# Expert layer: the 160-slot unit is fed one block at a time between blocks of the 64-slot units

## The chip, the cores and the metric

One core of one Trainium2 chip runs the whole program. The metric is the device time of one execution in microseconds (us). Before the change the median of 3 runs is 1689.62 us (1689.18 to 1689.63). The engines are named as the profile names them: PE (TensorE, the matrix engine; PEld is its loading of the stationary operand), DVE (VectorE), ACT (ScalarE), POOL (GpSimd) and SP (SyncE, which here only issues DMAs).

## The reference, cut to what matters

Two layers: each has a token mixer and a channel mixer. The second layer's channel mixer sends each of 256 tokens to 2 of 8 experts; each expert is a SwiGLU with three 1024 x 3584 matrices in float32. The change lies entirely in this part.

```python
def swiglu(y, wg, wu, wd):
    return (jax.nn.silu(y @ wg) * (y @ wu)) @ wd

def moe_swiglu(y, w_r, b_r, wg, wu, wd):
    logits = (y @ w_r).astype(jnp.float32) + b_r.astype(jnp.float32)
    top_val, top_idx = lax.top_k(logits, TOP_K)
    gates = jax.nn.softmax(top_val, axis=-1)
    combine = jnp.sum(jax.nn.one_hot(top_idx, N_EXPERTS, dtype=jnp.float32)
                      * gates[..., None], axis=-2).astype(y.dtype)
    out = jnp.zeros_like(y)
    for e in range(N_EXPERTS):
        out = out + combine[..., e:e + 1] * swiglu(y, wg[e], wu[e], wd[e])
    return out
...
f = ffn(modulate(rmsnorm(h, g_ffn_pre[i]), sh_f, sc_f))
h = h + gt_f * rmsnorm(f, g_ffn_post[i])
```

## The kernel before, in words

**Units.** The eight experts are worked through as eight units. Unit 0 is expert 0 with 32 slots for tokens; the other seven are sorted at run time by how many tokens chose them and get the fixed sizes of `SLOTS`: unit 1 has 160 slots, units 2 and 3 have 96, units 4 to 6 have 64, unit 7 has 32. In `SEQ` the first number is the rank (0 is the 160-slot unit, 3 to 5 the 64-slot units, 6 the last 32-slot unit, None is expert 0); below, units are named by their slots. Tokens beyond the slots are caught by code behind a branch that is not entered here.

**Blocks.** The 3584 hidden columns are cut into 7 blocks of 512 (`EB`). For each unit and block SP loads three tiles of 2 MiB ("quads"): two of gate and up weights (`eg`, `eu`), one of down weights (`ed`). So there are 56 blocks and 168 quads. `SEQ` lists runs of blocks, `(unit, first, end)`; `moe_items` (L1817) turns it into the order of the loads, always the gate and up quads of one block and then the down quad of the block before it. `t_load` (L475) issues them from SP in this order, each one when a buffer is free. There are eight buffers of this size (`NS`, `KEEP`); `REST` (L59) sets, at a step counted in blocks, how many of them are kept back for converted weights: 3 from step 7, none from step 28.

**Two ways to multiply.** 128 slots of the 160 go the "narrow" way: ACT and DVE split each weight quad into a rounded part and a rest (`t_hi`, `t_lo`, two further buffers a quad), and PE makes three fp32r products 128x512 for each (`mm3`), in `t_egu` (L1529) and `t_edown` (L1568). Slots in parts of 64 or 32 go the "wide" way, `t_xgu` (L1692) and `t_xdown` (L1733): raw float32 weights, two or four products side by side in the array, each shown as two MATMUL instructions. The last 32 of the 160 slots and the second part of each 96-slot unit are such parts of 32.

**Accumulators and finishes.** The sum over the blocks of one run of `SEQ` stays in PSUM banks (two for 128 slots, one for each wide part). At the end of the run a finish (`t_finish` L1589, `t_xfinish` L1758) splits it on ACT and DVE, multiplies it by the one-hot matrix on PE and adds it on DVE to the output `facc` by token. So a unit that is cut in three runs has three finishes. There are eight PSUM banks: `b:acc` accumulators, `b:g` gate and up, `b:m` (at most two) transposes and gathers, `b:x` the finish.

**The order on the engines.** The Python program plays a model of the engines (`Sched`, `Eng.product` holds the PE costs): of the tasks that could start it takes the one that starts first, with small biases. The order in which PE, ACT, DVE and SP get their instructions is that order. All engines' instructions are recorded on one line (L307), so rows are told apart by tile: `w` is a quad, `f`, `q`, `s` are smaller tiles, `b` a PSUM bank.

Of the kernel before, what the change touches and what calls it, by code (L numbers as in the profile page):

```python
# [17 lines left out]
F32R = mybir.dt.float32r  # L18
# [3 lines left out]
OP = mybir.AluOpType  # L22
# [7 lines left out]
EB = FF // 512  # L30
# [9 lines left out]
KEEP, SLACK, NEAR = 9, 4.0, 2  # L40
# [15 lines left out]
TABLE = 1.3  # L56
SC = {'PE': 1.0, 'ACT': 1.0, 'DVE': 1.0, 'POOL': 0.918, 'DMA': 1.0, 'NONE': 1.0}

REST = (0, ((6, 9, 0), (7, 9, 3), (28, 9, 0)))  # L59
ORD = ((1, 0, 5, 6, 7, 4, 3, 2, 8, 9, 10, 11), (5, 3, 2, 4, 6, 7, 9, 10, 8, 11, 0, 1))  # L60
CAP = (3, 1, 2, 4)
ADB, HI0 = -0.7, 5
# [8 lines left out]
JO = (3, 6, 1, 2, 5, 7, 4, 0)  # L71
WO = ((0, 2), (0, 1, 2, 3), (0, 1, 2, 3, 4, 6))

SEQ = ((None, 0, 7), (0, 0, 2), (3, 0, 7), (0, 2, 4), (4, 0, 7), (0, 4, 7), (5, 0, 7), (1, 0, 7), (6, 0, 4), (2, 0, 7), (6, 4, 7))


PE, ACT, DVE, POOL, DMA, NONE = "PE", "ACT", "DVE", "POOL", "DMA", "NONE"


def on(eng, *res, ev=()):  # L80

    return eng, res, tuple(ev)
# [213 lines left out]
class Eng:  # L296
# [17 lines left out]
    def product(self, op, out, a, n):  # L314
        if op == "transpose":
            return 0.11
        dt = a[1].dtype
        if dt == F32R and self.s.change and a[0].shape[0] < 128:
            return n / 2400 * a[0].shape[0] / 128 + 0.03
        if dt == F32R:  # L320
            return n / 2400 + 0.003 if n >= 256 else max(n / 600, 0.03)
        if out.shape[0] == 32:
            return max(n / 2300, 0.055)
        if out.shape[0] == 64 and n >= 256:
            return n / 1100
        return max(n / 600, 0.06) if dt == F32 else max(n / 2400, 0.03)
# [46 lines left out]
class Core:  # L373
# [1254 lines left out]
    def experts(self, units, seq):  # L1628

        go = self.sc.spawn  # L1630
        prev, state, near = None, {}, []
        for key, b0, b1 in seq:
            _, pos, base, slots, comb = units[key]
            down = []
            parts = self.parts(slots)
            for s, ws in parts:
                if b0 == 0:
                    out, hts = [[Event(), Event()], [Event() for _ in ws or [128]]], [Event() for _ in range(EB)]
                    ev = near if prev is None else [*near, *prev] if key >= NE else [*near, *prev, self.combed]
                    go(self.t_xgather(key, pos, base + s, ws, out, ev) if ws else self.t_gather(key, pos, base + s, [out[0], out[1][0]], ev), -0.3)  # L1640
                    prev = out[0]
                    state[key, s] = out, hts
                out, hts = state[key, s]
                acc = [Event() for _ in ws or [128]]
                down.append((self.t_xdown(key, b0, b1, ws, hts, acc) if ws else self.t_edown(key, b0, b1, hts, acc[0]), 0.0))
                for i, w in enumerate(ws or [128]):
                    finish, a = self.t_xfinish if ws else self.t_finish, (comb, acc[i], out[1][i], b1 == EB, *([w] if ws else []))
                    if (key, b0, b1) == seq[-1] and key < NE and (s, ws) == parts[-1] and i == len(ws or [128]) - 1:

                        self.last = lambda done, f=finish, a=a: f(*a, done)  # L1650
                    else:
                        down.append((finish(*a), -0.2))
            for b in range(b0, b1):
                for s, ws in reversed(parts):
                    out, hts = state[key, s]
                    go(self.t_xgu(key, b, ws, out[0], hts[b]) if ws else self.t_egu(key, b, out[0], hts[b]))
            if self.facc is None:
                self.facc = []
                go(self.t_facc([hts[3]]))
            near = [hts[max(b0, b1 - NEAR)]]  # L1660
            if (key, b0, b1) == seq[-1] and key < NE:
                go(self.t_gate([self.colev[1, 5], hts[max(b0, b1 - 3)]]))
            for t in down:
                go(*t)
# [93 lines left out]
    def t_xfinish(self, comb, acc, oht, last, w, done=None):  # L1758
        n = 8 * w
        fs = yield on(ACT, *["hr:xf"] * (w // 32), ev=[acc])  # L1760
        own = list(fs) if w == 64 else [fs]
        fs = self.pair(n, own)
        yield from self.g_split(acc.v[:, :n], *fs)
        self.sc.rel(acc.v)
        yield on(PE, ev=[oht, self.combed, self.faccev])
        comb = comb()
        ps = yield on(PE, *["b:x"] * 4)
        at = lambda t, q: (ps[2 * t + q], slice(0, 512)) if w == 64 else (ps[q], slice(t * 256, t * 256 + 256))
        for t in range(2):
            for i in range(2):  # L1770
                for q in range(128 // w):
                    r, (p, c) = slice(q * w, q * w + w), at(t, q)
                    self.pe.matmul(p[:, c], oht.v[r, t * 128:t * 128 + 128], fs[i][r, :], start=i == 0, stop=i == 1)
        for t in range(2):
            for q in range(128 // w):
                if q * n % 512 == 0:
                    yield on(DVE)
                f, (p, c) = self.facc[t][:, q * n:q * n + n], at(t, q)
                self.v.scalar_tensor_tensor(f, p[:, c], comb[:, t:t + 1], f, op0=OP.mult, op1=OP.add)
                if t or w == 64:  # L1780
                    self.sc.rel(p)
                if done and q * n % 512 + n == 512:
                    self.sc.set(done[t][q * n // 512])
        self.sc.rel(*own)
        if last:
            self.sc.rel(oht.v)
# [21 lines left out]
    @staticmethod  # L1808
    def seq():
        return [(0 if r is None else r + 1, b0, b1) for r, b0, b1 in SEQ]  # L1810

# [5 lines left out]
    def moe_items(self, seq, idx=None):  # L1817
# [16 lines left out]
        for n in range(len(steps) + 1):  # L1834
            if n < len(steps):
                e, b = steps[n]
                if idx is None:
                    it += [("rest", None, (r, q)) for m, r, q in REST[1] if n == m]
                for n2, k in enumerate(GU):
# [94 lines left out]
    def main(self):  # L1934
# [82 lines left out]
        self.sc.cap.update({("s", "raw"): 40, ("s", "hi"): 5, ("s", "lo"): 5})  # L2017
        self.sc.rest = REST[0]
        self.sc.change, self.sc.stay = CHG, STAY
# [136 lines left out]
```

## Time and profile before

| | |
|---|---|
| median of 3 runs | 1689.62 us |
| the profiled execution | 1687.98 us, of which the span in the trace 1685.9 us |
| PE busy | 1589.4 us (94%) |
| DVE, ACT busy | 775.9 us (46%), 528.6 us (31%) |
| moved by DMA | 497.30 MB, mean 295 GB/s |

How to read it: the expert layer is the second half of the span. By the trace, expert 0 (32 slots) ends at about 905 us, the 160-slot unit and the three 64-slot units fill 905 to 1360 us, and the 96-slot units with the last 32-slot unit fill the rest. The profiled execution is 1.64 us below the median of the runs. "Busy" of PE has modelled ends, so that consecutive matmuls overlap a little; intervals from start to start are the better price.

### The profile page before, as it was taken

The page shows a single profiled execution, that of the slowest core. Times are in us where ns is not written, and L with a number is a line of the kernel's source. Part 1 is how long each engine was busy: PE and PEld are TensorE (multiplying, and loading weights), DVE is VectorE, ACT ScalarE, POOL GpSimd, SP SyncE. Part 2 cuts the span into 40 slices and gives each one's busy share as a digit, 9 for nine tenths or more (in the row PEclk, how much of TensorE's full clock was granted, in tenths as well). Part 3 has the DMA queues.
Part 4 walks back from the last instruction along what each step waited for, and adds up shares of the span by engine and source line. Part 5 has one row for each costly group of instructions (what it writes and reads, how often), then busy time and mean ns, then how long its engine had stood idle before and what let it go on. Part 6 is the DMA issues. An engine that isn't in the chain of part 4 may idle for free. (4 is left out here: it accounts for less than half of the span.)

```text
span 1685.9 us, 25712 instructions
## 1 busy us (share of the span) xinstructions
PE 1589.4 (94%) x10580; PEld 1029.2 (61%) x10580; DVE 775.9 (46%) x1470; ACT 528.6 (31%) x951; POOL 26.2 (2%) x49
## 2 busy tenths in 40 slices
PE   6999999999999999999989999998999989989994
PEld 3776889888888888897646634642673333443342
DVE  4576688765644458987524512620841110021012
ACT  3477453323222235557415302410720000000001
POOL 0100000000000011000000000000000000000000
PEclk9999999999999999999989999999999999999997
DMA  9516435554544456864699999899889999999994
GB/s 370 212 37 238 167 133 209 180 171 152 178 159 163 171 187 208 317 245 142 261 374 418 385 427 425 367 426 428 331 338 428 426 426 427 391 425 427 426 425 180
DMA packets 71758, 497.30 MB, mean 295 GB/s; under 512 B 9004, under 2 KB 9136, under 8 KB 52048
## 3 DMA queue, kind: packets, MB, share of 16 engines
q1 hardware_dynamic: 68976, 490.76, 73.6%
q0 software_dynamic: 1792, 4.18, 0.7%
q8 instruction: 85, 1.39, 0.3%
q10 hardware_dynamic: 864, 0.62, 0.1%
q14 instruction: 41, 0.34, 0.1%
HBM read 494.49 MB, written 1.05 MB: 294 GB/s over the span
## 5 line engine op out<-in xcount | busy, mean ns | idle before, releaser
L307 PE MATMUL b<-s,s 128*128 128x512 f32 (+2 forms) x2864 | 579.7, 363 | 7.7 <-DVE s L307 6.5
L307 PEld LDWEIGHTS b<-s,s 128*128 128x128 f32 (+1 forms) x2864 | 460.1, 186 | 95.9 <-issue 9.6
L307 PE MATMUL b<-w,f 128*32 128x256 f32 (+1 forms) x2336 | 299.2, 480 | 28.9 <-DMA w<-in_w_gu_e_dram 28.9
L307 PE MATMUL b<-w,s 128*32 128x256 f32 (+2 forms) x1848 | 275.9, 439 | 9.1 <-DMA w<-in_w_gu_e_dram 9.1
L307 DVE TENSOR_TENSOR f<-f,b 128x256 f32<-128x256 f32 (+2 forms) x105 | 41.0, 393 | 518.3 <-ACT f L307 439.3
L307 ACT ACTIVATE f<-b 128x512 f32<-128x512 f32 (+4 forms) x183 | 82.3, 455 | 604.4 <-PE b L307 600.8
L307 PEld LDWEIGHTS b<-w,s 128*32 128x32 f32 (+2 forms) x1848 | 151.8, 138 | 123.3 <-issue 66.8
L307 PEld LDWEIGHTS b<-w,f 128*32 128x32 f32 (+1 forms) x2336 | 105.9, 124 | 197.9 <-issue 137.6
L307 ACT ACTIVATE s<-s 128x1024 fp32r<-128x1024 f32 (+2 forms) x173 | 179.0, 1050 | 146.8 <-PE b L307 84.4
L307 PE MATMUL b<-s,f 128*32 128x256 f32 (+1 forms) x1344 | 206.5, 401 | 16.7 <-DVE ones L774 8.6
L307 DVE TENSOR_TENSOR s<-s,s 128x1024 fp32r<-128x1024 f32 (+2 forms) x169 | 203.2, 1215 | 32.1 <-ACT s L307 27.9
L307 PEld LDWEIGHTS b<-s,f 128*32 128x32 f32 (+1 forms) x1344 | 145.0, 151 | 63.8 <-DMA s<-in_w_ada_dram 12.0
L307 DVE TENSOR_TENSOR w<-w,w 128x1024 fp32r<-128x1024 f32 x84 | 97.5, 1220 | 42.4 <-ACT w L307 42.3
L307 PE MATMUL b<-w,q 128*32 128x256 f32 (+1 forms) x880 | 111.5, 464 | 4.2 <-DMA w<-in_w_down_e_dram 2.2
L307 DVE SCALAR_TENSOR_TENSOR s<-s,cs,s 128x1024 f32<-128x1024 f32 x73 | 91.9, 1281 | 42.9 <-DMA s<-in_w_ada_dram 42.4
L307 ACT ACTIVATE w<-w 128x1024 fp32r<-128x1024 f32 x84 | 82.3, 1048 | 44.5 <-DMA w<-in_w_gu_e_dram 20.4
L307 PEld LDWEIGHTS b<-w,q 128*32 128x32 f32 (+1 forms) x880 | 39.3, 120 | 63.5 <-issue 53.2
L307 DVE TENSOR_TENSOR s<-b,s 128x512 f32<-128x512 f32 (+2 forms) x71 | 44.4, 629 | 54.5 <-ACT s L307 32.3
L307 PEld LDWEIGHTS b<-ident,f 128*128 128x128 f32 x313 | 34.2, 140 | 49.3 <-DVE f L307 22.5
L307 PE MATMUL b<-ident,f 128*128 128x128 f32 x313 | 55.3, 287 | 8.7 <-DVE f L307 4.6
L307 ACT ACTIVATE s<-b 128x512 f32<-128x512 f32 (+3 forms) x93 | 46.7, 524 | 46.9 <-PE b L307 44.9
L307 DVE SCALAR_TENSOR_TENSOR s<-b,utab,s 128x256 f32<-128x256 f32 (+1 forms) x88 | 44.2, 574 | 16.7 <-PE b L307 16.7
(162 smaller groups left out, 727.3 us busy)
## 6 DMA issues: line engine op xcount, KB each, us to landing
w<-in_w_gu_e_dram SPq DMA_DIRECT2D x101, 2048.0 KB, 20.9
w<-in_w_down_e_dram SPq DMA_DIRECT2D x52, 2048.0 KB, 21.7
s<-in_w_ada_dram SPq DMA_DIRECT2D x96, 512.0 KB, 4.8
s<-in_w_down_d_dram SPq DMA_DIRECT2D x56, 512.0 KB, 4.4
s<-in_w_gu_e_dram SPq DMA_DIRECT2D x44, 512.0 KB, 7.9
s<-in_w_gate_d_dram SPq DMA_DIRECT2D x28, 512.0 KB, 4.5
s<-in_w_up_d_dram SPq DMA_DIRECT2D x28, 512.0 KB, 3.9
s<-in_w_in_dram SPq DMA_DIRECT2D x24, 512.0 KB, 7.4
```

What stands on the lines that cost most here:

```text
L307: r = f(out, *a, **k)
```

## The change

The runs of `SEQ` are shorter: one block of the 160-slot unit stands between two or three blocks of the 64-slot units. The 160-slot unit keeps its accumulators over all seven blocks (`JOIN`) and is finished once instead of three times; each 64-slot unit is cut in three runs, with three finishes instead of one. The last 32-slot unit is cut in 2 + 2 + 3 blocks instead of 4 + 3, and comes earlier beside the 96-slot units. `t_xfinish` takes two banks `b:m` for each half of the tokens when the part has 64 slots, instead of four banks `b:x` at once. The reserve of buffers ends at step 32 instead of 28, and the planner's PE costs in this part are other ones.

```diff
-REST = (0, ((6, 9, 0), (7, 9, 3), (28, 9, 0)))
+REST = (0, ((6, 9, 0), (7, 9, 3), (32, 9, 0)))
...
-SEQ = ((None, 0, 7), (0, 0, 2), (3, 0, 7), (0, 2, 4), (4, 0, 7), (0, 4, 7), (5, 0, 7), (1, 0, 7), (6, 0, 4), (2, 0, 7), (6, 4, 7))
+JOIN = (1,)
+SEQ = ((None, 0, 7), (0, 0, 1), (3, 0, 3), (0, 1, 2), (3, 3, 6), (0, 2, 3), (3, 6, 7), (4, 0, 2), (0, 3, 4), (4, 2, 5), (0, 4, 5),
+       (4, 5, 7), (5, 0, 1), (0, 5, 6), (5, 1, 4), (0, 6, 7), (5, 4, 7), (6, 0, 2), (1, 0, 7), (6, 2, 4), (2, 0, 7), (6, 4, 7))
...
-        if dt == F32R and self.s.change and a[0].shape[0] < 128:
-            return n / 2400 * a[0].shape[0] / 128 + 0.03
+        if self.s.change:
+            if dt == F32R:
+                return n / 2400 * a[0].shape[0] / 128 + 0.016
+            if out.shape[0] < 128:
+                return n * out.shape[0] / 128 / 600 * 1.01
+            if n < 256:
+                return 0.225
...
+                if key in JOIN and b0:
+                    continue
+                d1 = EB if key in JOIN else b1
                 acc = [Event() for _ in ws or [128]]
-                down.append((self.t_xdown(key, b0, b1, ws, hts, acc) if ws else self.t_edown(key, b0, b1, hts, acc[0]), 0.0))
+                down.append((self.t_xdown(key, b0, d1, ws, hts, acc) if ws else self.t_edown(key, b0, d1, hts, acc[0]), 0.0))
...
-            near = [hts[max(b0, b1 - NEAR)]]
+            if key not in JOIN:
+                near = [hts[max(b0, b1 - NEAR)]]
...
-        ps = yield on(PE, *["b:x"] * 4)
-        at = lambda t, q: (ps[2 * t + q], slice(0, 512)) if w == 64 else (ps[q], slice(t * 256, t * 256 + 256))
-        for t in range(2):
-            for i in range(2):
-                for q in range(128 // w):
-                    r, (p, c) = slice(q * w, q * w + w), at(t, q)
-                    self.pe.matmul(p[:, c], oht.v[r, t * 128:t * 128 + 128], fs[i][r, :], start=i == 0, stop=i == 1)
...
+        for ts in ((0,), (1,)) if w == 64 else ((0, 1),):
+            ps = yield on(PE, *["b:m"] * 2 if w == 64 else ["b:x"] * 4)
+            for t in ts:
+                for i in range(2):
+                    for q, p in enumerate(ps):
+                        r = slice(q * w, q * w + w)
+                        self.pe.matmul(p[:, (t - ts[0]) * n:(t - ts[0]) * n + n], oht.v[r, t * 128:t * 128 + 128], fs[i][r, :],
+                                       start=i == 0, stop=i == 1)
+            for t in ts:
+                for q, p in enumerate(ps):
...
+                    self.v.scalar_tensor_tensor(f, p[:, (t - ts[0]) * n:(t - ts[0]) * n + n], comb[:, t:t + 1], f, op0=OP.mult, op1=OP.add)
+                    if t == ts[-1]:
+                        self.sc.rel(p)
```

## Rows read from the trace of the kernel before

**Rows 1.** The page, part 2: busy tenths in 40 slices of the span.
```profile
PE   6999999999999999999989999998999989989994
GB/s 370 212 37 238 167 133 209 180 171 152 178 159 163 171 187 208 317 245 142 261 374 418 385 427 425 367 426 428 331 338 428 426 426 427 391 425 427 426 425 180
```

**Rows 2.** Busy time by stretch: columns PE, PEld, DVE, ACT, POOL, clock, DMA share, GB/s.
```profile
905.00:960.00 55.00, 55.00 (x404) 37.09 (x397) 36.74 (x48) 26.61 (x35) 0.00 (x0) 0.98 0.95 387
960.00:1050.00 90.00, 84.34 (x432) 32.83 (x431) 17.06 (x28) 13.47 (x24) 0.00 (x0) 0.98 1.00 426
1050.00:1100.00 50.00, 50.00 (x332) 31.73 (x331) 30.52 (x39) 21.21 (x29) 0.00 (x0) 1.00 0.91 375
1100.00:1180.00 80.00, 73.73 (x366) 26.43 (x365) 10.29 (x21) 5.81 (x14) 0.00 (x0) 0.96 1.01 428
1200.00:1250.00 50.00, 50.00 (x361) 35.53 (x361) 34.28 (x44) 24.59 (x33) 0.00 (x0) 1.00 0.69 271
1250.00:1360.00 110.00, 102.34 (x546) 41.05 (x538) 18.56 (x36) 11.70 (x24) 0.00 (x0) 1.00 1.01 428
1450.00:1470.00 20.00, 20.00 (x230) 8.64 (x228) 0.98 (x3) 1.49 (x5) 0.00 (x0) 1.00 0.87 351
...
905.00:1360.00 455.00, 435.41 (x2559) 216.93 (x2551) 160.00 (x224) 115.85 (x172) 0.00 (x0) 0.99 0.95 399
...
1360.00:1659.00 299.00, 283.84 (x2811) 121.48 (x2811) 37.92 (x95) 23.49 (x66) 0.00 (x0) 0.98 0.99 420
```

**Rows 3.** The page, part 6: loads of weight quads, count, size, us to landing.
```profile
w<-in_w_gu_e_dram SPq DMA_DIRECT2D x101, 2048.0 KB, 20.9
```

**Rows 4.** PE in order of time: start, us to the last end, operation and count.
```profile
907.35 11.41 PE L307 MATMUL b<-w,s 128*128 128x512 f32 x48
918.69 1.93 PE L307 MATMUL b<-w,q 128*32 128x256 f32 x32
920.44 1.91 PE L307 MATMUL b<-w,f 128*32 128x256 f32 x32
922.28 0.66 PE L307 MATMUL b<-ident,f 128*128 128x128 f32 x4
...
984.45 1.89 PE L307 MATMUL b<-w,q 128*64 128x512 f32 x8
986.27 0.44 PE L307 MATMUL b<-ident,f 128*128 128x128 f32 x2
986.64 7.09 PE L307 MATMUL b<-w,f 128*64 128x512 f32 x32
```

**Rows 5.** Groups by shape from 905 to 1670 us: count, busy, mean ns, idle before.
```profile
L307 PE MATMUL b<-w,s 128*128 128x512 f32 x504 | 122.7, 398 | 0.0
...
L307 PE MATMUL b<-f,q 32*128 32x256 f32 x117 | 6.5, 317 | 4.2 <-ACT f L307 4.0
L307 PE MATMUL b<-s,q 128*128 128x512 f32 x24 | 6.3, 406 | 0.0
L307 PE MATMUL b<-f,q 64*128 64x512 f32 x40 | 5.9, 415 | 0.0
```

**Rows 6.** PE in order of time, where the tile forms alternate, 1216 to 1226 us.
```profile
1216.43 1.64 PE L307 MATMUL b<-w,s 128*128 128x512 f32 x6
...
1217.99 3.66 PE L307 MATMUL b<-w,f 128*32 128x256 f32 x64
...
1221.59 4.47 PE L307 MATMUL b<-w,s 128*128 128x512 f32 x18
```

**Rows 7.** Waits, 1195 to 1262 us: us in total, times, longest.
```profile
PEld b L307 <- issue: 9.2, 21, 0.8
```

**Rows 8.** Waits, 905 to 1360 us: us in total, times, longest.
```profile
PEld b L307 <- DVE f L307: 13.8, 19, 0.8
PE b L307 <- DMA w<-in_w_gu_e_dram: 17.2, 10, 4.1
```

**Rows 9.** SP's own waits, 905 to 1360 us.
```profile
SPq L509 <- PE b L307: 323.1, 82, 14.0
```

**Rows 10.** PE in order of time at the end: the last down block.
```profile
1661.99 1.93 PE L307 MATMUL b<-w,q 128*32 128x256 f32 x32 [1.76 <-SPq L1797]
```

More of the change, by code (lines that the diff above doesn't have):

```diff
@@ L1643, in experts @@
                 out, hts = state[key, s]
+                if key in JOIN and b0:
+                    continue
+                d1 = EB if key in JOIN else b1
                 acc = [Event() for _ in ws or [128]]
-                down.append((self.t_xdown(key, b0, b1, ws, hts, acc) if ws else self.t_edown(key, b0, b1, hts, acc[0]), 0.0))
+                down.append((self.t_xdown(key, b0, d1, ws, hts, acc) if ws else self.t_edown(key, b0, d1, hts, acc[0]), 0.0))
                 for i, w in enumerate(ws or [128]):
-                    finish, a = self.t_xfinish if ws else self.t_finish, (comb, acc[i], out[1][i], b1 == EB, *([w] if ws else []))
+                    finish, a = self.t_xfinish if ws else self.t_finish, (comb, acc[i], out[1][i], d1 == EB, *([w] if ws else []))
                     if (key, b0, b1) == seq[-1] and key < NE and (s, ws) == parts[-1] and i == len(ws or [128]) - 1:
@@ L1766, in t_xfinish @@
         comb = comb()
-        ps = yield on(PE, *["b:x"] * 4)
-        at = lambda t, q: (ps[2 * t + q], slice(0, 512)) if w == 64 else (ps[q], slice(t * 256, t * 256 + 256))
-        for t in range(2):
-            for i in range(2):
-                for q in range(128 // w):
-                    r, (p, c) = slice(q * w, q * w + w), at(t, q)
-                    self.pe.matmul(p[:, c], oht.v[r, t * 128:t * 128 + 128], fs[i][r, :], start=i == 0, stop=i == 1)
[L1774 to L1783, printed above, removed]
+        for ts in ((0,), (1,)) if w == 64 else ((0, 1),):
[8 more added lines that the diff above has]
+                for q, p in enumerate(ps):
+                    if q * n % 512 == 0:
+                        yield on(DVE)
+                    f = self.facc[t][:, q * n:q * n + n]
+                    self.v.scalar_tensor_tensor(f, p[:, (t - ts[0]) * n:(t - ts[0]) * n + n], comb[:, t:t + 1], f, op0=OP.mult, op1=OP.add)
+                    if t == ts[-1]:
+                        self.sc.rel(p)
+                    if done and q * n % 512 + n == 512:
+                        self.sc.set(done[t][q * n // 512])
         self.sc.rel(*own)
```

## The prediction

> **What bounds the kernel now.** Read the slices of the span first [rows 1]: in the second half, the expert layer, PE is busy at 8 to 9 tenths and DMA moves 418 to 428 GB/s in most slices, but not in all. So two engines share the bound, and the next view has to show which of them waits where. By stretch [rows 2] the two take turns. Where the 160-slot unit runs (905 to 960, 1050 to 1100, 1200 to 1250) PE has no idle time at all and DMA drops to 387, 375 and 271 GB/s. Where a 64-slot unit runs (960 to 1050, 1100 to 1180, 1250 to 1360) DMA is full at 426 to 428 and PE idles 5.7, 6.3 and 7.7 us; its waits there are for weights [rows 8], while SP's waits are nearly all for PE, which frees the buffers [rows 9].
>
> The prices say why. A block is three quads of 2 MiB [rows 3], 6.29 MB, 14.7 us at 427 GB/s. On PE, from start to start [rows 4], a 160-slot block costs 11.3 us (48 narrow products, gate and up), half of that again for down (5.7), twice 1.75 for the wide gate and up (64 instructions), 1.75 for wide down and 0.6 for transposes: 22.9 us, 8.2 more than its load. A 64-slot block costs 7.1 + 3.6 + 0.4 = 11.1 us, 3.6 less than its load. Two or three 160-slot blocks in a row put PE 16 to 25 us behind, the buffers fill, DMA stops; then seven 64-slot blocks make PE wait.
>
> Summed up: from 905 to 1360 us, 28 blocks that need 28 x 14.7 = 412 us of DMA take 455 us. DMA lacks (427 - 399) x 455 / 427 = 29.8 us there and (427 - 351) x 20 / 427 = 3.6 us at 1450 to 1470: 33.4 us. PE idles 455 - 435.4 = 19.6 us in this stretch and 299 - 283.8 = 15.2 us after it: 34.8 us. Neither is all to be had, but the time lies there.
>
> **The change part by part.** *Runs of one block.* One 160-slot block and three of 64 slots need 22.9 + 3 x 11.1 = 56.2 us of PE and 58.9 us of DMA, so within each group of four the excess of the one is paid by the other, and seven groups use up exactly the 7 and 21 blocks. The look-ahead is five quads (eight buffers, three kept back until step 32), 24.5 us, more than the 8.2 us that one 160-slot block puts PE behind. This takes away both waits as far as the rest of the work on PE allows, so PE's work is summed next.
>
> *Finishes.* Two of three finishes of the 160-slot unit go. In PE time: 2 x 8 products at 6.3 / 24 = 0.26 us and 2 x 16 at 6.5 / 117 = 0.056 us [rows 5], 4.2 + 1.8 = 6.0 us less. The 64-slot units have nine finishes instead of three: 6 x 8 products at 5.9 / 40 = 0.15 us, 7.1 us more; the last 32-slot unit has one more, 0.9 us. The splits and adds of these finishes lie on ACT and DVE, which are busy 115.9 and 160.0 of the 455 us [rows 2]: taken as hidden. If they were not, each finish would hold PE for one wait as in [rows 8], 13.8 / 19 = 0.73 us, 5 us in all.
>
> *More changes of tile form on PE.* 160-slot and 64-slot runs met 5 times in this stretch and will meet 13 times; where they meet, gate and up of the one alternate with down of the other, about four changes a time, so some 32 more. What one costs: six narrow products before a change took 1.56 us from start to start and 64 wide ones before the next 3.60 us [rows 6], against 1.42 and 3.50 us at the steady price of [rows 4]: 0.14 and 0.10 us. From above it is bounded by the loading of weights, which stood still 9.2 / 21 = 0.44 us each time without a reason shown [rows 7]; from below by 0, as PE itself shows no gap from 1200 to 1250. I take 0.14, the measured step: 4.5 us (0 to 14). The Trainium skill, page "TensorEngine Tiling (Array Packing)", section Tiling Modes, speaks against the change here: it says that a change of tiling mode, not of tile alone, drains the engine. It gives no price; with the upper bound as the drain the gain below would be 10 us smaller, and the 0.14 us say that most of the drain is hidden.
>
> *Two banks in place of four for a 64-slot finish, accumulators held throughout.* The 160-slot unit holds three of eight PSUM banks, now also while 64-slot blocks run. A 64-slot block then has its own accumulator and four others, a 160-slot block three for gate and up and one for transposes. No instruction is added. From below it may gain a little, since a finish no longer waits for four free banks; from above see the slower rival. I take 0.
>
> *Planner's costs and the reserve until step 32.* No instruction is added; they move only the order. Three buffers held back four steps longer shorten the look-ahead from 8 to 5 quads for blocks that are now interleaved. Bounds -3 to +3 us, 0 taken. SP's queue is in order: a late buffer holds back every load behind it, which is the second case below.
>
> *PE's clock.* It was granted 0.96 on the mean from 1100 to 1180 and 0.98 at 960 to 1050, the stretches with waits, that is the lower of its two levels for 8% and 4% of the time. Fewer waits can give back at most half of 6.4 + 3.6 us. I take 0, as these slow products lay beside waits for DMA.
>
> **The sum.** PE in the stretch of 28 blocks: 435.4 - 6.0 + 7.1 + 4.5 = 441 us. Some waiting will stay, between 0 (1200 to 1250) and 19.6 us; I take 3, since the groups are balanced to 5%. That is 444 in place of 455 us: 11 us. Behind it PE enters the 96-slot units with weights already there, since DMA, if it runs on, brings 444 / 14.7 = 30.2 blocks and the buffers hold 5 to 8 quads, 1.7 to 2.7 blocks, beyond the 28. Of the 15.2 us of PE waits after 1360, about half should go; the last blocks still wait for the last weights, and the down block at the end has its own 1.8 us wait [rows 10]. With the extra finish: 7 us. Together 18 us. The sum by DMA must agree: of 33.4 us missing, some 4 stay in the stretch, the 3.6 at 1450 to 1470 stay, and about 4 come new at the second 96-slot unit, where only two 32-slot blocks lie before it: 33.4 - 11.6 = 22 us. The smaller one governs. 1687.98 - 18 = 1670.0 us for the profiled execution, 1.64 more for the median: 1671.6 us. I predict 1671.5.
>
> **The rivals.** *The buffers still run full (1680 us, 20%).* A 160-slot quad needs its own buffer and two more for the split, and SP cannot pass it. Today DMA loses 29.8 / 7 = 4.3 us for each 160-slot block; if half of it stays, 15 us, then 33.4 - 15 - 7.6 leaves 11 us, less the tail that PE then brings: 8 to 10 us. For it: SP waited 323 us for PE in this stretch [rows 9]. Against it: the loss falls on runs of two and three such blocks, and grows with the run (387, 375, 271 GB/s).
>
> *PSUM becomes the bound (1705 us, 15%): slower.* In a 64-slot block only four banks are left for gate and up, transposes and finishes, and a 64-slot finish wants both `b:m` banks that transposes and gathers use. PE is in order, so a product that waits for a bank stops everything behind it, then SP's loads. One exposed wait for DVE cost 0.73 us [rows 8]. If each of 28 blocks loses one such wait and a form change of 0.44 us more, about 1.2 us, the sum is 33.6 - 18 = 15.6 us slower. It decides from 18 / 28 = 0.64 us a block on. Against it: PE waited for DVE only 19 times in 28 blocks, and the 160-slot blocks already ran with three accumulators held.
>
> *The order on PE does not change as `SEQ` does (within 0.2%, 8%).* PE's order is the planner's, not the list's; but the loads follow the list, so PE would then wait for them. Beyond my bounds, more than 28 us gained (all of PE's 34.8 us less the 6.5 added): 2%; a fault elsewhere that makes it slower: 1%.
>
> **How the numbers follow.** The forecast with its own range, 1661 to 1678 us (a gain of 12 to 28: form changes from 14 to 0 us, remaining waits 0 to 8), has 54%. About 0.2%, 3.4 us, is what can be told from no change. Faster: 54 + 20 + 2 = 76%; same 8%; slower 15 + 1 = 16%. The range goes from 1659 to 1692: it leaves out most of the slower case and next to nothing below.
>
> **What would show it.** Right: between 905 and 1350 us DMA above 415 GB/s with no slice under 350, PE idle under 8 us there, eight fp32r products of the narrow finish instead of 24, the last load some 18 us earlier and the same tail behind it. Wrong: many PE waits for DVE or ACT in 64-slot blocks (PSUM), or DMA still at 250 to 390 GB/s in steps of about 60 us (buffers), or PE slower at the same counts (form changes).

## The result and the profile after

The changed kernel takes 1664.34 us (median of 4 runs, 1662.94 to 1667.74) against 1689.4 us: ratio 0.9858, interval 0.984 to 0.9876, 25 us faster. The forecast was 1671.5 us, with its own range from 1661 to 1678. The profiled execution of the changed kernel took 1667.74 us, the longest of its four runs; against the profiled one before (1687.98 us) that is 20.2 us, so all comparisons of traces below explain 20 us and not 25; the other 5 are the spread of the runs on both sides.

The slices of the span, after (compare [rows 1]): from the 22nd slice to the last but one DMA is at 418 to 427 GB/s, with two dips left (397 and 391), and PE is at 8 or 9 tenths throughout.

```profile
PE   5999999999999999999998999999999999999995
GB/s 374 214 39 228 164 152 165 214 144 180 170 167 156 174 168 227 259 330 155 152 344 418 421 427 427 426 426 397 427 391 419 427 426 425 425 426 426 426 422 181
```

The same by stretch, with the columns of [rows 2]: PE, PEld, DVE, ACT, POOL, clock, DMA share, GB/s.

```profile
905.00:960.00 55.00, 54.37 (x392) 30.39 (x392) 21.68 (x31) 15.70 (x23) 0.00 (x0) 1.00 0.99 416
960.00:1050.00 90.00, 87.61 (x508) 42.60 (x506) 33.00 (x38) 26.88 (x38) 0.00 (x0) 1.00 1.01 426
1050.00:1100.00 50.00, 50.00 (x315) 24.75 (x312) 23.30 (x33) 14.53 (x20) 0.00 (x0) 1.00 1.01 426
1100.00:1180.00 80.00, 77.83 (x413) 37.21 (x415) 26.05 (x30) 21.42 (x31) 0.00 (x0) 0.96 0.98 412
1180.00:1260.00 80.00, 78.72 (x465) 39.74 (x459) 29.74 (x42) 18.47 (x28) 0.00 (x0) 1.00 0.97 408
1260.00:1350.00 90.00, 88.19 (x545) 41.71 (x543) 30.74 (x49) 19.78 (x32) 0.00 (x0) 1.00 1.00 423
...
1430.00:1450.00 20.00, 20.00 (x198) 8.03 (x197) 1.13 (x3) 1.54 (x4) 0.00 (x0) 1.00 1.01 428
...
905.00:1350.00 445.00, 436.71 (x2624) 216.39 (x2624) 164.50 (x220) 116.78 (x172) 0.00 (x0) 0.99 0.99 418
905.00:1640.00 735.00, 719.62 (x5364) 337.44 (x5366) 204.63 (x319) 140.23 (x237) 0.00 (x0) 0.99 1.00 420
```

No stretch swings between "DMA full, PE waits" and "PE full, DMA at 271" any more. DMA lacks (427 - 420) x 735 / 427 = 12.0 us from 905 to 1640, of them 9.4 up to 1350; before, the prediction's sum gave 33.4. PE idles 445 - 436.7 = 8.3 us up to 1350, the end of the interleaved part, and 15.4 us up to 1640; before it was 19.6 up to 1360 and 34.8 up to 1659, the same points of the work. PE's waits for gate and up weights in the interleaved part have shrunk from 17.2 us [rows 8] to 1.7, and DVE is now what PE waits for most (before, PE waited for DVE 1.0 us in all from 905 to 1659 us):

```profile
PE b L310 <- DVE f L310: 4.5, 5, 1.4
PE b L310 <- DMA w<-in_w_gu_e_dram: 1.7, 4, 0.6
```

How the blocks alternate on PE, after (start, us to the last end, operation, count): one block of narrow gate and up (48 products `w,s` 128*128), then 64-slot products (`w,q` and `w,f` 128*64), then the narrow down in pieces (18 of its 24) among them.

```profile
1157.87 11.37 PE L310 MATMUL b<-w,s 128*128 128x512 f32 x48
1169.17 1.08 PE L310 MATMUL b<-w,q 128*64 128x512 f32 x4
...
1173.07 6.18 PE L310 MATMUL b<-w,f 128*64 128x512 f32 x28
...
1183.09 4.46 PE L310 MATMUL b<-w,s 128*128 128x512 f32 x18
1187.48 3.65 PE L310 MATMUL b<-w,f 128*64 128x512 f32 x16
```

The end is the same work: the last down products, here two blocks of them, stop at 1643.92 + 3.66 = 1647.6 us, before at 1661.99 + 1.93 = 1663.9 [rows 10]; that is 16.3 us. From there to the end of the span it is 18.4 us instead of 22.0: the last finish now starts on ACT 0.1 us after these products and started 4.7 us after them before, by the trace without a reason shown.

```profile
1643.92 3.66 PE L310 MATMUL b<-w,q 128*32 128x256 f32 x64
```

Counted from the loads, the end is the same. The weight loads run out in the slice from 1655 to 1660 us before (first line) and in that from 1635 to 1640 after (second line), 20 us earlier, and the span is 1685.9 - 1666.0 = 19.9 us shorter.

```profile
1655.00:1660.00 5.00, 5.00 (x81) 3.01 (x73) 0.29 (x1) 1.04 (x3) 0.00 (x0) 1.00 0.73 310
1635.00:1640.00 5.00, 5.00 (x68) 2.62 (x70) 3.34 (x7) 0.60 (x1) 0.00 (x0) 1.00 0.76 321
```

### The profile page after: what moved, and what is told of

It reads as the page before. It is cut to its first block, busy times and chain, and to the rows that moved or that the text cites. A ratio compares the mean times of both kernels' runs of the same rounds, so it can differ in the third digit from the quotient of the medians.

```text
span 1666.0 us, 25796 instructions
## 1 busy us (share of the span) xinstructions
PE 1593.7 (96%) x10596; PEld 1029.8 (62%) x10596; DVE 786.0 (47%) x1479; ACT 528.9 (32%) x952; POOL 26.1 (2%) x49
## 5 line engine op out<-in xcount | busy, mean ns | idle before, releaser
L310 PE MATMUL b<-w,f 128*32 128x256 f32 (+1 forms) x2336 | 293.5, 468 | 5.7 <-DMA w<-in_w_gu_e_dram 5.7
L310 PE MATMUL b<-w,s 128*32 128x256 f32 (+2 forms) x1848 | 272.4, 437 | 3.1 <-DMA w<-in_w_gu_e_dram 2.7
L310 ACT ACTIVATE s<-s 128x1024 fp32r<-128x1024 f32 (+2 forms) x173 | 179.0, 1050 | 147.2 <-PE b L310 84.0
L310 PE MATMUL b<-w,q 128*32 128x256 f32 (+1 forms) x880 | 115.9, 482 | 4.3 <-DMA w<-in_w_down_e_dram 4.3
L310 PEld LDWEIGHTS b<-w,q 128*32 128x32 f32 (+1 forms) x880 | 39.7, 123 | 60.7 <-issue 49.4
L310 DVE SCALAR_TENSOR_TENSOR s<-b,utab,s 128x512 f32<-128x512 f32 (+1 forms) x96 | 52.7, 610 | 24.2 <-PE b L310 24.0
```

The costliest lines, as they stand in the source:

```text
L310: r = f(out, *a, **k)
```

## The experiments

Theory A: the gain is the alternation of single 160-slot blocks with 64-slot blocks, so that neither DMA nor PE waits. Rivals: B, fewer narrow finishes with kept accumulators; C, the planner's new costs; D, the new order at the end. Each run has its own comparison with the kernel before (1688.9 to 1691.4 us there), so two runs are best compared by what each gains or loses against it.

**The old list of runs in the changed kernel**

```diff
-SEQ = ((None, 0, 7), (0, 0, 1), (3, 0, 3), (0, 1, 2), ...
+SEQ = ((None, 0, 7), (0, 0, 2), (3, 0, 7), (0, 2, 4), (4, 0, 7), (0, 4, 7), ...
-REST = ... (32, 9, 0)
+REST = ... (28, 9, 0)
```

> The changed kernel with the old list of runs and the old step at which the buffer reserve ends; accumulators kept, finish with two banks and new planner costs stay. Theory A (the gain is the alternation of single 160-slot blocks with 64-slot blocks): 1680 to 1692 us, DMA again at 250 to 390 GB/s where two or three 160-slot blocks follow each other. Theory B (fewer narrow finishes and kept accumulators): below 1675. Theory C (planner costs): below 1675 as well, with PE in another order.

1709.04 us, ratio 1.0097 (1.0076 to 1.0118): 18 us slower than before. Neither accumulators nor costs carry the gain by themselves, so B and C fall in their plain form. But A foresaw at most 1692; something in the other edits costs time once the runs are long again. PE waits 13.7 us for DVE up to 1350 us here; the runs with kept accumulators alone and with new costs alone, below, show what such waits are.

**No kept accumulators in the changed kernel**

```diff
-JOIN = (1,)
+JOIN = ()
```

> The changed kernel without the kept accumulators: the 160-slot unit is finished after each of its seven blocks. Theory A: PE gets six narrow finishes more, 6 x 3.0 = 18 us of PE work, of which the PE waits that are left (8 us up to 1350) hide a part: 1670 to 1684 us. Theory B: all of the gain goes, 1685 or more. If the held PSUM banks were what limits the changed kernel: 1664 or less.

1692.65 us, ratio 1.0009 (0.9998 to 1.0019): alternation without kept accumulators gains nothing. Against the changed kernel that is 27 us lost (25 gained there, 1.6 lost here) for six finishes of the 160-slot unit. By PE's work 18 us were to be paid at most. More work shows on another engine: DVE is busy 205.18 us up to 1350 instead of 164.50, and PE waits 7.7 us for it instead of 4.5; how the 9 us beyond the 18 divide was not taken apart.

```profile
905.00:1350.00 445.00, 430.95 (x2567) 218.66 (x2561) 205.18 (x298) 123.76 (x183) 0.00 (x0) 0.98 0.93 392
```

A finish of that unit costs DVE two splits of 0.69, one of 0.42, four adds of 0.745 and eight of 0.476 us, 8.6 us in all; six are 52 us. (Counts and mean ns, DVE of this run, 905 to 1650 us; adds of 512 columns, adds of 256, splits of 512 and of 256.)

```profile
L310 DVE SCALAR_TENSOR_TENSOR s<-b,utab,s 128x512 f32<-128x512 f32 x68 | 47.4, 744 | 14.8 <-PE b L310 14.8
L310 DVE SCALAR_TENSOR_TENSOR s<-b,utab,s 128x256 f32<-128x256 f32 x80 | 32.5, 476 | 15.8 <-PE b L310 15.7
...
L310 DVE TENSOR_TENSOR s<-b,s 128x512 fp32r<-128x512 f32 x21 | 14.4, 686 | 21.8 <-ACT s L310 21.6
...
L310 DVE TENSOR_TENSOR f<-b,f 128x256 fp32r<-128x256 f32 x11 | 4.6, 418 | 9.0 <-ACT f L310 9.0
```

**The old planner costs in the changed kernel**

```diff
-        if self.s.change:
-            if dt == F32R:
-                return n / 2400 * a[0].shape[0] / 128 + 0.016
...
+        if dt == F32R and self.s.change and a[0].shape[0] < 128:
+            return n / 2400 * a[0].shape[0] / 128 + 0.03
```

> The changed kernel with the old PE costs in the planner. Theory A: within 4 us of 1664, since no instruction differs. Theory C: 1675 or more.

1666.27 us, ratio 0.9865 (0.9833 to 0.9896): beside the other edits the costs give nothing that can be told. C falls.

**Two of three narrow products**

```diff
+    def mm2(self, out, lh, ll, rh, rl, start, stop):
+        mm = self.pe.matmul
+        mm(out, lh, rh, start=start, stop=False)
+        mm(out, lh, rl, start=False, stop=stop)
...
-                self.mm3(p, ys[0][:, s], ys[1][:, s], wh[:, w], wl[:, w], k == 0, k == KC - 1)
+                self.mm2(p, ys[0][:, s], ys[1][:, s], wh[:, w], wl[:, w], k == 0, k == KC - 1)
...
```

> The changed kernel with two of the three products for the 128-slot part (the low part of the activations times the high part of the weights is left out): 168 matmuls less, 168 x 0.236 = 39.7 us less PE work, the same loads. If DMA bounds the changed kernel from the 160-slot unit on, as its full rate says: only the 9 us that DMA still misses there can go, 1653 to 1661 us. If PE bounds it: 1630 to 1645.

1659.3 us, ratio 0.981 (0.9784 to 0.9836). Of 39.7 us less PE work, by count, only 5 come out (7 by the two comparisons). DMA now runs at 425 GB/s up to 1350, and PE waits 15.2 us for gate and up weights there:

```profile
905.00:1350.00 445.00, 418.97 (x2566) 186.60 (x2569) 170.84 (x234) 118.07 (x178) 0.00 (x0) 0.99 1.01 425
```

So from 905 us on the changed kernel is within some 5 to 7 us of what its loads allow. Both engines were near their bound, DMA nearer.

**Kept accumulators alone in the kernel before**

```diff
+JOIN = (1,)
...
+                if key in JOIN and b0:
+                    continue
+                d1 = EB if key in JOIN else b1
```

> The kernel before with one part of the change: the 160-slot unit keeps its accumulators over its three runs (old list of runs, old planner costs, old finish with four banks). PE saves two narrow finishes, 6.0 us. The three held PSUM banks cost nothing (forecast): 1680 to 1690 us. If held banks and old runs do not go together, which is what the run with the old list hints at (1709): 1697 to 1712, with PE waiting for DVE while 64-slot blocks run.

1697.62 us, ratio 1.0046 (1.0029 to 1.0063): 8.7 us slower although PE has 6 us less to do. PE waits for DVE 14.2 us in 4 waits up to 1350 us, up to 6.2 us each.

```profile
PE b L309 <- DVE f L309: 14.2, 4, 6.2
```

Two of these waits, 6.17 and 5.99 us, are the same picture. Here is the first. PE's transpose (`ident,f`) needs the product of gate and up (`f<-f,b`, 0.28 us on DVE), and that needs ACT's part (`f<-b`, 0.26 us). Both short instructions stand behind four splits of weights, 3.90 us on ACT and 4.62 us on DVE.

```profile
1064.55 3.90 ACT L309 ACTIVATE w<-w 128x1024 fp32r<-128x1024 f32 x4
...
1065.82 4.62 DVE L309 TENSOR_TENSOR w<-w,w 128x1024 fp32r<-128x1024 f32 x4
1068.36 0.26 ACT L309 ACTIVATE f<-b 128x128 f32<-128x128 f32 x1
1070.36 0.28 DVE L309 TENSOR_TENSOR f<-f,b 128x128 f32<-128x128 f32 x1
...
1070.79 0.45 PE L309 MATMUL b<-ident,f 128*128 128x128 f32 x1 [6.17 <-DVE f L309]
```

**New planner costs alone in the kernel before**

```diff
+        if self.s.change:
+            if dt == F32R:
+                return n / 2400 * a[0].shape[0] / 128 + 0.016
...
```

> The kernel before with the new planner costs alone. Forecast's reading (costs only move the order, -3 to +3): 1687 to 1694. If the costs are what made the old list slow (1709): 1700 or more. If they are a gain in themselves: 1680 or less.

1713.2 us, ratio 1.0132 (1.0112 to 1.0152): 24 us slower with the same work in another order. The trace shows where (start, us, engine, operation; this run, 926 to 941 us): PE is through at 931.75 and its next instruction, the transpose of the gate product (`ident,f`), starts at 940.09, after 8.34 us. The product of gate and up (`f<-f,b` 128x128, 0.29 us) stands on DVE behind four splits of weights (`w<-w,w`, 4.62 us), and these run beside ACT's four.

```profile
931.11 0.64 PE L307 MATMUL b<-w,f 128*32 128x256 f32 x8
932.50 0.25 ACT L307 ACTIVATE f<-b 128x128 f32<-128x128 f32 x1
933.60 3.90 ACT L307 ACTIVATE w<-w 128x1024 fp32r<-128x1024 f32 x4 [0.84 <-DMA w<-in_w_down_e_dram]
...
935.12 4.62 DVE L307 TENSOR_TENSOR w<-w,w 128x1024 fp32r<-128x1024 f32 x4
939.66 0.29 DVE L307 TENSOR_TENSOR f<-f,b 128x128 f32<-128x128 f32 x1
...
940.09 0.45 PE L307 MATMUL b<-ident,f 128*128 128x128 f32 x1 [8.34 <-DVE f L307]
```

So a product that PE needs was put behind work for the next quad. Five waits for DVE sum to 16.7 us up to 1350; this one and one of 6.2 us, also behind splits, make up most of it. Around the second, DMA falls to 183 GB/s (before, [rows 2], 375 from 1050 to 1100):

```profile
1080.00:1100.00 20.00, 13.56 (x102) 10.59 (x101) 15.14 (x23) 7.84 (x11) 0.00 (x0) 0.83 0.47 183
```

**The old order at the end in the changed kernel**

```diff
-SEQ = (..., (6, 0, 2), (1, 0, 7), (6, 2, 4), (2, 0, 7), (6, 4, 7))
+SEQ = (..., (1, 0, 7), (6, 0, 4), (2, 0, 7), (6, 4, 7))
```

> The changed kernel with the old order at the end (the last 32-slot unit in 4 + 3 blocks, the first 96-slot unit ahead of it). The stall of DMA that before had at 1450 to 1470 (3.6 us) should come back, a little more since PE enters the 96-slot units behind: 1664 to 1674. If the new order at the end carries the gain: 1680 or more.

1670.43 us, ratio 0.9893 (0.9876 to 0.9909), some 6 us above the changed kernel. DMA stops again at 1430 to 1450 (253 GB/s). D carries a part of the gain, not all of it.

**The new order at the end alone in the kernel before**

```diff
-SEQ = (..., (1, 0, 7), (6, 0, 4), (2, 0, 7), (6, 4, 7))
+SEQ = (..., (6, 0, 2), (1, 0, 7), (6, 2, 4), (2, 0, 7), (6, 4, 7))
```

> The kernel before with the new order at the end alone. It removes at most the stop of DMA at 1450 to 1470 (3.6 us): 1684 to 1690. Undoing the same part in the changed kernel cost 6 us (1670.4 against 1664.3); if that is a gain by itself: 1681 to 1684.

1686.45 us, ratio 0.9964 (0.995 to 0.9978): 5 us by itself. The stop of DMA at 1450 to 1470 [rows 2] is gone in it, as in the changed kernel (423 GB/s there):

```profile
1450.00:1470.00 20.00, 20.00 (x185) 7.84 (x185) 1.13 (x3) 1.54 (x4) 0.00 (x0) 1.00 0.99 419
```

**The new list alone in the kernel before**

```diff
-SEQ = ((None, 0, 7), (0, 0, 2), (3, 0, 7), ...
+SEQ = ((None, 0, 7), (0, 0, 1), (3, 0, 3), (0, 1, 2), ...
-REST = ... (28, 9, 0)
+REST = ... (32, 9, 0)
```

> The kernel before with the new list of runs alone (and the reserve until step 32): the 160-slot unit is finished after each of its seven blocks, old planner costs, old finish with four banks. If alternation gains by itself and only the finishes eat it, as the run without kept accumulators says (1692.7): 1686 to 1698. If four banks at once for a 64-slot finish hurt more in the new list: 1698 or more. If alternation without the other edits gains: 1682 or less.

1707.97 us, ratio 1.0092 (1.0069 to 1.0114): 16.5 us slower. PE waits 20.5 us for DVE in 11 waits up to 1350; 5.2 us of it, in four waits, lie before products of 64-slot finishes, the rest almost all before transposes that need a product of gate and up. The same list without kept accumulators, but with new costs and the finish of two banks, lost only 1.6 us (above). So one of these two is worth 15 us there, though neither shows beside kept accumulators; which one was not tried.

```profile
PE b L308 <- DVE f L308: 20.5, 11, 4.2
```

**The old finish of 64 slots in the changed kernel**

```diff
-        for ts in ((0,), (1,)) if w == 64 else ((0, 1),):
-            ps = yield on(PE, *["b:m"] * 2 if w == 64 else ["b:x"] * 4)
...
+        ps = yield on(PE, *["b:x"] * 4)
...
```

> The changed kernel with the old finish of 64 slots, which asks for four banks at once. Forecast's reading (nothing from the banks): 1662 to 1668. If the two banks are needed beside the three held ones, a finish waits until four of five banks are free, eight or nine times: 1672 or more.

1665.7 us, ratio 0.9845 (0.982 to 0.987): two banks or four make no difference that can be told, although the 88 products of these finishes keep PE busy 14.0 us here and 18.7 in the changed kernel, where they come four at a time instead of eight (this run, 905 to 1650 us):

```profile
L310 PE MATMUL b<-f,q 64*128 64x512 f32 x88 | 14.0, 428 | 2.6 <-DVE f L310 2.0 <-ACT f L310 0.6
```

**Look-ahead of three quads instead of five in the changed kernel**

```diff
-REST = (0, ((6, 9, 0), (7, 9, 3), (32, 9, 0)))
+REST = (0, ((6, 9, 0), (7, 9, 5), (32, 9, 0)))
```

> The changed kernel with five of the eight weight buffers kept back instead of three, so that loads run three quads ahead (14.7 us) instead of five. Forecast's reading: one 160-slot block puts PE 8.2 us behind its loads, three quads still cover this, so little is lost: 1664 to 1672. If look-ahead is what the gain hangs on (the second case of the forecast): 1680 or more, DMA stopping at each 160-slot block.

1665.88 us, ratio 0.9845 (0.9823 to 0.9867), with 419 GB/s up to 1350 (418 in the changed kernel). Alternation needs no long look-ahead, and the forecast's second case (buffers still run full) falls.

**Kept accumulators for the 64-slot units too**

```diff
-JOIN = (1,)
+JOIN = (1, 4, 5, 6)
...
-            if key not in JOIN:
+            if key != 1:
```

> The changed kernel, and the 64-slot units keep their accumulators too: six finishes of 64 slots less, 6 x 1.2 = 7 us of PE work, and no PSUM bank more held at a time. If PE waits and DMA stops are what is left (DMA misses some 9 us from the 160-slot unit on): 1657 to 1664. If DMA already bounds it: 1662 to 1666. If held accumulators cost order: 1668 or more.

1659.0 us (1658.27 to 1660.27), ratio 0.9824 (0.9807 to 0.984): about 5 us below the changed kernel, the best of all, touching its interval. DVE falls to 149.8 us up to 1350 and DMA is at its full rate for the whole part:

```profile
905.00:1350.00 445.00, 433.08 (x2686) 219.67 (x2689) 149.79 (x203) 115.61 (x172) 0.00 (x0) 1.00 1.00 425
1350.00:1620.00 270.00, 262.93 (x2516) 108.74 (x2508) 35.08 (x87) 20.50 (x55) 0.00 (x0) 1.00 1.01 426
```

**Together.** The edits don't add. The list alone costs 16.5 us, kept accumulators alone 8.7, the costs alone 24, and the end alone gains 5; yet all of them but the costs gain 24.8. So theory A is shown in part only: alternation gains together with kept accumulators, and neither does alone. What goes with the losses is DVE: where single edits lose, PE waits 14 to 21 us for DVE up to 1350, in the changed kernel 4.5, with joined 64-slot units 2.0. That a product of gate and up behind splits on ACT and DVE stops PE is shown in two runs; why the planner puts it there after one edit and not after another was not tried and stays open. The buffers' reserve until step 32 was changed only with the list, never apart from it.

## Why the prediction was right, point by point

**Alternation removes both waits: right.** DMA's lack went from 33.4 to 12.0 us, as summed (11.6 were to stay), and the loads end 20 us earlier with the same time behind them, as the prediction's signs said (18 us). That the sum met so well is luck in part: 9.4 of the 12 lie before 1350, where 4 were forecast, and 2.6 after, where 7.6 were. PE idles 8.3 us in the stretch, where the sum had 3 and the sign "under 8".

**"The smaller one governs": the step that was off.** The sum by DMA gave 22 us, 1667.6 us for the median; the sum by PE gave 18 and was taken. The profiled runs differ by 20.2 us, the medians by 25. Taking 39.7 us of PE work away moves the time by only 5 to 7 us, and the span shrank as the loads did, so DMA's sum was the one to follow. On PE the last product came 16.3 us earlier, near the 18, but its terms were off both ways. Form changes were to cost 4.5 us; but the steady products are no dearer after than before: 504 narrow ones 122.7 us [rows 5], after 122.3, as the first row of PE by shape shows (count, busy, mean ns; changed kernel, 905 to 1650 us).

```profile
L310 PE MATMUL b<-w,s 128*128 128x512 f32 x504 | 122.3, 398 | 0.3 <-DVE w L310 0.3
...
L310 PE MATMUL b<-f,q 64*128 64x512 f32 x88 | 18.7, 475 | 4.2 <-DVE f L310 3.5 <-ACT f L310 0.7
...
L310 PE MATMUL b<-s,q 128*128 128x512 f32 x8 | 2.1, 405 | 0.0
```

The 64-slot finishes were too cheap: 7.1 us more were forecast, and their products (second row) went from 5.9 us [rows 5] to 18.7, 12.8 more. Of that 4.7 come with the new form of the finish (14.0 with the old one), which was put at nothing because it adds no instruction. And the 3.6 us stop of DMA at 1450 to 1470 was kept in the forecast. The new order at the end removed it (423 GB/s there), and is worth 5 to 7 us by two runs. I had listed the edit and given it no term for a gain.

**PE's clock at nothing: too low.** Before, 16 products of a 64-slot block took 6.37 us behind a wait for weights (granted clock 0.50 from 1150 to 1155 us, the lower level, 1.2 GHz), and the next 16 like them 3.60 us:

```profile
1151.14 6.37 PE L307 MATMUL b<-w,f 128*64 128x512 f32 x16 [4.07 <-DMA w<-in_w_gu_e_dram]
...
1158.20 3.60 PE L307 MATMUL b<-w,f 128*64 128x512 f32 x16
```

Such a wait cost 2.8 us more than its own length. After, the longest wait for gate and up weights up to 1350 is 0.6 us, and the 64-slot weight products keep PE busy 383.6 us from 905 us on, before 388.3. The lower clock is not gone: after two waits of a finish for ACT and DVE it lies on what follows them (0.50 from 1120 to 1125 us).

**Finishes: right in count, wrong in price and in what hides them.** PE's part came as counted (narrow ones 8 products instead of 24; 64-slot ones 88 instead of 40), in the rows above. DVE's part was "taken as hidden" because DVE was busy only 160 of 455 us. Over the stretch that mean is true; within a 160-slot block it is not (30.5 of 50 us at 1050 to 1100, [rows 2]). Exposed waits came to 4.5 us for DVE and 0.7 for ACT up to 1350, which is the 5 us that the prediction had named and left out. (The 0.73 us that it priced them by were waits of PEld in [rows 8]; PE itself was busy beside them.) It was no more, because two finishes of 8.6 us went and six of 3.7 us came (a split of 0.69 and four adds of 0.745): DVE 160.0 before in the stretch, 164.5 after. Six finishes more of the large kind cost 27 us, and six less of the small kind gave 5.

**Costs of the planner, -3 to +3 us: right here (+1.9), wrong as a bound.** The same edit alone costs 24 us in the old list.

**Banks at nothing: right for the time** (+1.4 us with four banks, within the runs' spread). **The rival of PSUM** was a wrong name for a true danger: held accumulators with long runs do lose 8.7 us with PE waiting for DVE; in the alternating list they do not. That free banks were what lacked was not shown. **The rival of full buffers** fell with three quads of look-ahead. What spoke for it was no sign: SP waits for PE as long in the changed kernel as before (323.1 us up to 1360, [rows 9], four fifths of its waits), while DMA runs full.

```profile
SPq L517 <- PE b L310: 331.4, 84, 15.9
```

**The rival of an unchanged order on PE** falls by the alternating rows above.

## What to carry to other kernels

Where two engines are bound in turn by different stages, put the stages together in small pieces at the ratio at which their excesses cancel. Here the gain was about the sum of DMA's stops that went (21 us, against 20 between the profiled runs), and the engine nearer to its bound over the whole part gave the better forecast. Small pieces multiply what is done at the end of a piece, so keep accumulators over them, and price that work on the engine that does it within the piece, not by its mean over the stretch. Try such edits together: three of the four tried alone were slower.

## What the runs showed that I had not expected

An order alone costs 24 us of 1689: one 0.29 us product behind four splits on DVE stopped PE for 8.3 us, and PE's waits for DVE sum to 16.7 us up to 1350. A look-ahead of three 2 MiB loads is as good as five (1665.9 against 1664.3 us). One core moved 425 GB/s from memory for 445 us on end, with PE busy 433 us of them (64-slot units joined).
